# Which engine makes the low halves: two transformer blocks on one core of a Trainium2 chip

## The chip, the cores and the metric

The program runs on one core of one Trainium2 chip, as a single launch. The metric is the device time of the launch in microseconds, the median of several runs. The engines are named as the profile names them: PE (TensorE, matmuls; PEld is its weight load), DVE (VectorE), ACT (ScalarE), POOL (GpSimd) and SP (SyncE, which issues nearly all DMAs).

## What is computed

256 tokens of width 1024 go through three layers, all in float32. Layer one is a chunked gated linear attention and a product-key mixture of experts ("peer"); layer two is a sliding-window attention with sinks and a second peer; layer three adds retention and a latent attention ("mix") and a routed mixture of 32 experts ("moe"). Cut to what matters here:

```python
def first_block(...):
    for l in range(2):
        h = modulate(x, norm_g[l, 0], sh1, sc1)
        y = gla_mixer(h, ...) if l < 1 else swa_sink_attention(h, ...)
        x = x + g1 * y
        y = peer(modulate(x, norm_g[l, 1], sh2, sc2), ...)   # 16384 experts, 8 heads, top 16
        x = x + g2 * y

def token_mixer(u, ...):                        # third layer
    proj = u @ w_in
    rq, rk = apply_rope(rq, *ret_rope), apply_rope(rk, *ret_rope)   # x1*c - x2*s, x2*c + x1*s
    y_ret = (silu(rg) * head_norm(retention(rq, rk, rv))) @ w_ret_o
    y_mla = mla(...) @ w_mla_o
    return (sigmoid(gate_ret) * y_ret + sigmoid(gate_mla) * y_mla) @ w_out
```

## The kernel before

**Low and high halves.** Most large products are made of three matmuls (`mm3`, lines 258 to 260): both operands are split into a high half, which is the float32 value cast to fp32r, and a low half, the float32 rest. Weights come from HBM in pages of 128x1024 (512 KB; some are 512, 704 or 768 wide). `fill` (line 229, through `split`, line 224) loads a page into one of four `raw` buffers; ACT casts it to `hi` (L226), and DVE or POOL subtracts to make `lo` (L227). `hi` and `lo` have three buffers each. So the raw buffer of a page is free, and its successor's load can start, only when the low half is made, and a new page can be cast only when PE is done with the page three before.

**Which engine makes a low half.** `self.lo_every = 2` says that every second page's low half goes to POOL and the other to DVE. In the sums over peer's experts (two loops of 128 pages in each peer layer) the kernel sets it by itself: 0 while POOL scatters gates, 2 otherwise. Everywhere else the initial 2 holds: in the projections of gated attention, of peer's queries, of window attention and of the whole mix.

**The order of work** is written out by hand: the program runs under a manual schedule, so each engine executes its instructions in the order in which the code issues them. `proj_T` and `proj_nat` walk the pages of a weight; at page k they call `page()`, which fills ahead so that pages k+1 and k+2 are split, then issue the matmuls; the last two pages of a projection are taken together. `drive` gives, after each page, one step to a side chain (the attention's small products, rotations, retention) and one `tick` to the background gemv that makes later modulations (L488 and L490 on DVE, buffer `gacc`).

**The other places on POOL.** `affine` (line 422) modulates four 256-column chunks and splits them: for the second bank of a pair DVE casts (L440) and the two low halves with j != k are POOL's (L444). In gated attention POOL makes `kt` (L699). In mix, `turn256` rotates queries and keys: four products on DVE (L1496 to L1499, 128x256) and the difference and sum on POOL (L1500, L1501); `norm` multiplies retention's output by the gate on POOL (L1675, 128x1024); `merge` has POOL make the low halves of the merged activations (L227 with `act<-g`).

Of the kernel before, what the change touches and what calls it, by code (L numbers as in the profile page):

```python
# [10 lines left out]
F32 = mybir.dt.float32  # L11
# [5 lines left out]
OP = mybir.AluOpType  # L17
# [142 lines left out]
class Prog:  # L160
    def __init__(self, ctx, tc, A, pages):
        self.ctx, self.tc, self.A, self.nc = ctx, tc, A, tc.nc
        nc = self.nc
        self.cp = ctx.enter_context(tc.tile_pool(name="cp", bufs=1))
        self.dp = ctx.enter_context(tc.tile_pool(name="dp", bufs=1, space=bass.MemoryType.DRAM))
        self.wp = ctx.enter_context(tc.tile_pool(name="wp", bufs=1))
        self.ps = ctx.enter_context(tc.tile_pool(name="ps", bufs=1, space=PSUM))
        self.pages, self.taken, self.split_at, self.ready = pages, 0, 0, []
        self.landed, self.early = [], 0
        self.lo_every, self.nlo, self.busy = 2, 0, False  # L170
        self.S, self.mc = {}, {}
        self.bg, self.rate, self.credit, self.due = iter(()), 0.0, 0.0, ()
        self.elist, self.eready, self.eat, self.ep, self.rt = list(ELIST), [], 0, {}, None
        self.wr = None
        self.acc, self.gnext, self.graw = None, None, self.raw

        self.gd = [self.dp.tile([128 * 128 * 128, 1], F32, name=f"gd{l}") for l in range(2)]
        self.zq = iter(())
        self.dg, self.s1 = [None, None], [None, None]
        self.ss, self.ss1 = [[None, None] for _ in range(2)], [[None, None] for _ in range(2)]  # L180
        ncol = A["cols"].shape[1]
        self.cols = self.cp.tile([128, ncol], F32, name="cols")
        nc.sync.dma_start(self.cols, A["cols"])
        C = self.cols
        ca = self.cp.tile([128, 16], F32, name="ca")
        nc.scalar.activation(ca, C[:, 0:16], AF.Silu)
        self.cact = self.cp.tile([128, 16, 32], F32, name="cact")
        nc.vector.tensor_copy(self.cact, ca[:, :, None].to_broadcast([128, 16, 32]))
        self.X = self.x8()
        nc.sync.dma_start(self.X, A["x"].rearrange("b p d -> p b d"))  # L190
        self.ident, self.iota = self.const(self.cp, 0, 2)
        self.ng = [[C[:, 16 + 16 * l + 8 * i:24 + 16 * l + 8 * i] for i in range(2)] for l in range(2)]
        self.kvng, self.n1, self.n2 = C[:, 48:56], C[:, 56:64], C[:, 64:72]
        self.qn, self.kvn, self.glan = C[:, 72:75], C[:, 75:77], C[:, 77:79]
        self.fng = C[:, 79:87]
        self.ones = self.cp.tile([128, 128], F32, name="ones")
        nc.vector.memset(self.ones, 1.0)
        self.nhalf = self.cp.tile([128, 8], F32, name="nhalf")
        nc.vector.memset(self.nhalf, -0.5)
        self.rope = self.rope_tab(self.cp)  # L200
# [221 lines left out]
    def affine(self, i, banks, a, sh, hi, lo, nch=8):  # L422

        nc = self.nc
        t = self.tmp()
        at = lambda x, j, k: x[:, (2 * j + k) * 256:(2 * j + k) * 256 + 256]

        def aff(j, k):
            c, o, b = 2 * (i + j) + k, at(t, j, k), banks[j][:, k * 256:k * 256 + 256]
            if j and sh is None:  # L430
                nc.scalar.activation(o, b, AF.Copy, scale=a(c))
            elif j:
                nc.scalar.activation(o, b, AF.Identity, scale=a(c), bias=sh(c))
            elif sh is None:
                nc.vector.tensor_scalar(o, b, a(c), None, op0=OP.mult)
            else:
                nc.vector.tensor_scalar(o, b, a(c), sh(c), op0=OP.mult, op1=OP.add)

        def high(j, k):
            (nc.vector.tensor_copy if j else nc.scalar.copy)(hi[:, 2 * (i + j) + k], at(t, j, k))  # L440

        def low(j, k):
            c = 2 * (i + j) + k
            (nc.gpsimd if j != k else nc.vector).tensor_tensor(lo[:, c], at(t, j, k), hi[:, c].bitcast(F32), OP.subtract)  # L444

        for f, j, k in ((aff, 0, 0), (high, 0, 0), (aff, 1, 0), (aff, 0, 1), (low, 0, 0), (high, 0, 1), (low, 0, 1),
                        (aff, 1, 1), (high, 1, 0), (low, 1, 0), (high, 1, 1), (low, 1, 1)):
            if 2 * (i + j) + k < nch and j < len(banks):
                f(j, k)
# [138 lines left out]
    def gla(self):  # L588
        nc, A, tc = self.nc, self.A, self.tc
        with tc.tile_pool(name="gp", bufs=1) as gp:  # L590
# [14 lines left out]
            hi, lo = act = self.act8(), self.act8()  # L605
# [77 lines left out]
            raw = gp.tile([128, 8, 256], F32, name="qkraw")  # L683
# [12 lines left out]

            def scores():
                nc.vector.scalar_tensor_tensor(qt, raw[:, :4], 128.0 ** -0.5, E[0], op0=OP.mult, op1=OP.mult)
                nc.gpsimd.tensor_tensor(kt, raw[:, 4:], E[1], OP.mult)  # L699
                nc.vector.tensor_tensor(kd, raw[:, 4:], E[2], OP.mult)  # L700
                yield
                kk = gp.tile([128, 4, 128], F32, name="kk")
                for h in range(4):
                    nc.vector.tensor_scalar(kk[:, h, :64], kd[:, h, :64], dec[:, h, 1:2], None, op0=OP.mult)
                    nc.vector.tensor_scalar(qq[:, h, 64:], qt[:, h, 192:], dec[:, h, 2:3], None, op0=OP.mult)
                nc.gpsimd.tensor_copy(kk[:, :, 64:], kd[:, :, 64:128])
                nc.gpsimd.tensor_copy(qq[:, :, :64], qt[:, :, 128:192])
                yield
                pk = self.bank("tp")
                for h in range(4):  # L710
                    nc.tensor.transpose(pk[:, h * 128:h * 128 + 128], kk[:, h], self.ident)
                nc.scalar.copy(kn.rearrange("p a b -> p (a b)"), pk)
                yield
                for tb in range(2):
                    t = slice(tb * 128, tb * 128 + 128)
                    p1, p2 = self.bank("tp"), self.bank("tp")
                    for h in range(4):
                        nc.tensor.matmul(p1[:, h * 128:h * 128 + 128], lhsT=kt[:, h, t], rhs=qt[:, h, t],
                                         start=True, stop=True)
                        nc.tensor.matmul(p2[:64, h * 128:h * 128 + 128], lhsT=kd[:, h, tb * 128:tb * 128 + 64],  # L720
                                         rhs=qt[:, h, t], start=True, stop=True)
                    p1v = p1.rearrange("p (h c) -> p h c", h=4)
                    p2v = p2.rearrange("p (h c) -> p h c", h=4)
                    nc.vector.copy_predicated(sT[:, tb], tri[:, None, :].bitcast(I32).to_broadcast([128, 4, 128]), p1v)
                    nc.vector.tensor_copy(sT[:64, tb, :, 64:], p2v[:64, :, 64:])
                    yield
# [59 lines left out]
    def peer(self, l, mcname, rate=0.0, due=(), fuse=False):  # L786
        nc, A, tc = self.nc, self.A, self.tc
        with tc.tile_pool(name=f"ap{l}", bufs=1) as ap:
# [298 lines left out]
            for i in range(128):  # L1087
# [34 lines left out]
                held = []  # L1122
                self.tick()
            self.acc, self.gnext, self.graw = None, None, self.raw


    def rope_tab(self, pool):
# [229 lines left out]
    def mix(self, due=(), fuse=False):  # L1357
        nc, A, tc = self.nc, self.A, self.tc
        tt = nc.vector.tensor_tensor
        with tc.tile_pool(name="mo", bufs=1) as mo:  # L1360
# [32 lines left out]
            def merge(i):  # L1393
                tt(pair(g2[1], i), bk[i], pair(g2[1], i), OP.mult)
                tt(pair(g2[0], i), pair(g2[0], i), pair(g2[1], i), OP.add)
                self.split(pair(g2[0], i), pair(mh, i), pair(ml, i), nc.gpsimd)

            G = self.gbcast("c2", self.rt.tile([128, 1024], F32, name="G", tag="G"))
            bk = []
# [11 lines left out]
    def branches(self, mi, big, act, oh, ol, gate, due, fuse, rest):  # L1411
# [79 lines left out]
        def turn256(x):  # L1491

            for h in range(4):
                x1, x2 = x[:, 2 * h], x[:, 2 * h + 1]
                w4 = self.tmp().rearrange("p (a t) -> p a t", a=4)
                tt(w4[:, 0], x1, rcos, OP.mult)  # L1496
                tt(w4[:, 1], x2, rsin, OP.mult)
                tt(w4[:, 2], x2, rcos, OP.mult)
                tt(w4[:, 3], x1, rsin, OP.mult)  # L1499
                nc.gpsimd.tensor_tensor(x1, w4[:, 0], w4[:, 1], OP.subtract)  # L1500
                nc.gpsimd.tensor_tensor(x2, w4[:, 2], w4[:, 3], OP.add)  # L1501
                yield

        for dst, side in ((qr, latents()), (kr, turn256(qr))):
# [141 lines left out]
        def retention():  # L1646
# [23 lines left out]
            def norm(nb):  # L1670
                r = self.rstd(mv[:, 4 * nb:4 * nb + 4, 1], 1, 4)
                for h in range(4):
                    nc.vector.tensor_scalar(y[:, nb, h], y[:, nb, h], mv[:, 4 * nb + h, 0:1], r[:, h:h + 1],
                                            op0=OP.subtract, op1=OP.mult)
                nc.gpsimd.tensor_tensor(y[:, nb], y[:, nb], sg[:, nb], OP.mult)  # L1675

            for nb in range(2):
                for h in range(4):
# [408 lines left out]
```

## Time and profile before

| | |
|---|---|
| time of three runs, median | 2559.11 us (2558.82 to 2561.59) |
| profiled execution, its own time | 2556.15 us |
| its span on the core | 2554.1 us, granted TensorE clock 0.98 |
| PE busy | 2383.4 us, 93% |
| DVE, ACT, POOL busy | 64%, 49%, 47% |

The stages by time in the span, from the windows and the lines that belong to each: gated attention 0 to 178, peer's queries to about 216 and its sums to about 1005; window attention to 1140, the second peer's queries to about 1195 and its sums to 1955; mix to 2318, the expert layer to the end. Busy time of an engine counts the time from an instruction's start to its end, so an instruction that stands still inside counts as busy. A wait is put down to the instruction whose end released the one that waited.

### The profile page before, as it was taken

Reading aid. Unit: us, or ns where it says so; the run is one execution under the profiler, and the core shown is the slowest. Engines: PE = TensorE matmul, PEld = TensorE weight load, DVE = VectorE, ACT = ScalarE, POOL = GpSimd, SP = SyncE. Lnnn points to the kernel's source line nnn. Section 1 sums busy time; section 2 is a strip of 40 time slices with the busy share of each in tenths; the row PEclk is TensorE's granted clock in tenths of the full one; section 3 lists DMA queues with packets and bytes.
Section 4 is the critical chain, followed back from the end, with each engine's and each line's share of the span. In section 5 each row is a group of like instructions: output and inputs, shape, how many; then the busy total and the mean of one; then the engine's idle time right before and its main releaser. Section 6 shows DMA issues by size and latency. Waiting matters only on the chain. (4 is left out here: it accounts for less than half of the span.)

```text
span 2554.1 us, 40763 instructions
## 1 busy us (share of the span) xinstructions
PE 2383.4 (93%) x15378; PEld 2034.7 (80%) x15378; DVE 1638.6 (64%) x2884; ACT 1241.8 (49%) x2172; POOL 1194.1 (47%) x676
## 2 busy tenths in 40 slices
PE   7989999999999999889999999999998889798886
PEld 5669999999787877669999999788886878785321
DVE  3772898777478885663898777466665666643211
ACT  2544454698444444554454797444444445332101
POOL 2443487783454544443478774444445543341000
PEclk9999999999999999999999999999999999998999
DMA  8647777765688885548677765688885446588997
GB/s 322 207 168 255 215 185 186 178 149 132 221 306 302 292 314 173 182 155 278 208 189 183 181 141 141 215 273 280 282 286 170 156 161 214 170 334 331 408 409 305
DMA packets 244846, 591.26 MB, mean 231 GB/s; under 512 B 56852, under 2 KB 108948, under 8 KB 244132
## 3 DMA queue, kind: packets, MB, share of 16 engines
q1 hardware_dynamic: 207780, 588.45, 68.3%
q0 software_dynamic: 36864, 0.15, 3.7%
q8 instruction: 123, 2.02, 0.3%
q14 instruction: 79, 0.65, 0.1%
HBM read 568.45 MB, written 20.05 MB: 230 GB/s over the span
## 5 line engine op out<-in xcount | busy, mean ns | idle before, releaser
L226 ACT CAST hi<-raw 128x1024 fp32r<-128x1024 f32 (+3 forms) x690 | 714.4, 1040 | 624.7 <-PE b_acc L260 391.1
L227 POOL TENSOR_TENSOR lo<-raw,hi 128x1024 fp32r<-128x1024 f32 (+2 forms) x238 | 608.8, 2558 | 836.2 <-ACT hi L226 805.3
L227 DVE TENSOR_TENSOR lo<-raw,hi 128x1024 fp32r<-128x1024 f32 (+2 forms) x452 | 589.5, 1305 | 513.0 <-ACT hi L226 496.9
L260 PE MATMUL b_acc<-act,lo 128*128 128x256 f32 x2624 | 748.5, 285 | 20.2 <-POOL lo L227 11.2
L258 PE MATMUL b_acc<-act,hi 128*128 128x256 f32 x2624 | 754.3, 287 | 9.8 <-ACT act L440 4.4
L259 PE MATMUL b_acc<-act,hi 128*128 128x256 f32 x2624 | 746.8, 285 | 2.1 <-DVE act L444 2.0
L954 POOL DMA_INDIRECT gd<-rg x256 | 473.8, 1851 | 133.5 <-issue 73.4
L260 PEld LDWEIGHTS b_acc<-act,lo 128*128 128x128 f32 x2624 | 507.4, 193 | 24.1 <-POOL lo L227 13.3
L258 PEld LDWEIGHTS b_acc<-act,hi 128*128 128x128 f32 x2624 | 507.6, 193 | 13.2 <-ACT act L440 5.1
L259 PEld LDWEIGHTS b_acc<-act,hi 128*128 128x128 f32 x2624 | 507.7, 193 | 2.7 <-DVE act L444 2.7
L259 PE MATMUL b_acc<-lo,act 128*128 128x512 f32 (+1 forms) x1200 | 469.8, 391 | 20.2 <-DVE lo L227 16.0
L258 PE MATMUL b_acc<-hi,act 128*128 128x512 f32 (+1 forms) x1200 | 471.8, 393 | 4.5 <-ACT hi L226 4.4
L260 PE MATMUL b_acc<-hi,act 128*128 128x512 f32 (+1 forms) x1200 | 467.9, 390 | 0.3 <-POOL act L227 0.3
L259 PEld LDWEIGHTS b_acc<-lo,act 128*128 128x128 f32 x1200 | 226.5, 189 | 72.2 <-DVE lo L227 20.7
L258 PEld LDWEIGHTS b_acc<-hi,act 128*128 128x128 f32 x1200 | 226.4, 189 | 62.0 <-issue 8.9
L260 PEld LDWEIGHTS b_acc<-hi,act 128*128 128x128 f32 x1200 | 226.8, 189 | 47.1 <-POOL act L227 0.7
L1058 ACT ACTIVATE A<-b_acc 128x256 f32<-128x256 f32 (+1 forms) x256 | 90.5, 354 | 242.2 <-PE b_acc L260 234.3
L490 DVE SCALAR_TENSOR_TENSOR A<-A,cact 128x1024 f32<-128x1024 f32 x70 | 153.1, 2187 | 3.4 <-DMA A<-in_modw_dram 3.1
L346 POOL TENSOR_TENSOR rs<-rm,nhalf 128x1 f32<-128x1 f32 (+2 forms) x20 | 13.3, 664 | 255.4 <-DVE rm L380 228.7
L1010 ACT ACTIVATE X<-cst,IT 128x128 f32<-128x128 f32 x256 | 88.4, 398 | 0.1
L227 DVE TENSOR_TENSOR act<-A,act 128x1024 fp32r<-128x1024 f32 x62 | 79.8, 1288 | 0.0
L1920 ACT ACTIVATE hd<-b_gv 128x256 f32<-128x256 f32 x8 | 3.1, 384 | 149.8 <-PE b_gv L1918 149.8
(528 smaller groups left out, 2724.9 us busy)
## 6 DMA issues: line engine op xcount, KB each, us to landing
raw<-in_pu_dram SPq DMA_DIRECT2D x256, 512.0 KB
raw<-in_pv_dram SPq DMA_DIRECT2D x256, 512.0 KB
ew<-in_mw_dram SPq DMA_DIRECT2D x87, 512.0 KB
A<-in_modw_dram SPq DMA_DIRECT2D x64, 512.0 KB
raw<-in_win_dram SPq DMA_DIRECT2D x48, 512.0 KB
gr<-in_modw_dram SPq DMA_DIRECT2D x40, 512.0 KB
raw<-in_modw_dram SPq DMA_DIRECT2D x40, 512.0 KB
ez<-in_mw_dram SPq DMA_DIRECT2D x35, 512.0 KB
```

Source lines behind the costliest of these rows:

```text
L226: nc.scalar.copy(hi, src)
L227: (eng or nc.vector).tensor_tensor(lo, src, hi.bitcast(F32), OP.subtract)
L258: nc.tensor.matmul(out, lhsT=lh, rhs=rh, start=start, stop=False, **kw)
L259: nc.tensor.matmul(out, lhsT=lh, rhs=rl, start=False, stop=False, **kw)
L260: nc.tensor.matmul(out, lhsT=ll, rhs=rh, start=False, stop=stop, **kw)
L346: nc.gpsimd.tensor_tensor(y, m, self.nhalf[:, :width], OP.pow)
L490: nc.vector.scalar_tensor_tensor(acc, r, self.cact[:, k, 0:1], acc, op0=OP.mult, op1=OP.add)
L954: d = nc.gpsimd.indirect_dma_start(out=gtab, out_offset=bass.IndirectOffsetOnAxis(ap=row[:, h, j:j + 1], axis=0), in_=gate[:, h, j:j + 1], ...
L1010: nc.scalar.activation(ob[:, 1, j], self.iota, AF.Abs, scale=-1.0, bias=IT[:, 1, t:t + 1])
L1058: nc.scalar.activation(W[:, i, :(128 if tq else 256)], o[:, :(128 if tq else 256)], AF.Gelu)
L1920: nc.scalar.activation(hd[:, 0], b[:, :256], AF.Silu)
```

## The change

Nine lines. `lo_every` starts at 0 and is set back to 0 when a peer layer ends, so that pages outside the two loops over experts have their low half on DVE. In `affine` all casts are ACT's and all low halves DVE's. `kt`, the rotations' difference and sum, retention's gate product and merge's low halves move from POOL to DVE. The loops over experts keep their setting. POOL keeps the root (`pow`), the diagonal for the turned modulation, memsets, small copies and the scatter.

```diff
@@ Prog.__init__
-        self.lo_every, self.nlo, self.busy = 2, 0, False
+        self.lo_every, self.nlo, self.busy = 0, 0, False
@@ affine
         def high(j, k):
-            (nc.vector.tensor_copy if j else nc.scalar.copy)(hi[:, 2 * (i + j) + k], at(t, j, k))
+            nc.scalar.copy(hi[:, 2 * (i + j) + k], at(t, j, k))
         def low(j, k):
             c = 2 * (i + j) + k
-            (nc.gpsimd if j != k else nc.vector).tensor_tensor(lo[:, c], at(t, j, k), hi[:, c].bitcast(F32), OP.subtract)
+            nc.vector.tensor_tensor(lo[:, c], at(t, j, k), hi[:, c].bitcast(F32), OP.subtract)
@@ gla, scores
-                nc.gpsimd.tensor_tensor(kt, raw[:, 4:], E[1], OP.mult)
+                nc.vector.tensor_tensor(kt, raw[:, 4:], E[1], OP.mult)
@@ peer, at its end
             self.acc, self.gnext, self.graw = None, None, self.raw
+            self.lo_every = 0
@@ mix, merge
-                self.split(pair(g2[0], i), pair(mh, i), pair(ml, i), nc.gpsimd)
+                self.split(pair(g2[0], i), pair(mh, i), pair(ml, i))
@@ branches, turn256
-                nc.gpsimd.tensor_tensor(x1, w4[:, 0], w4[:, 1], OP.subtract)
-                nc.gpsimd.tensor_tensor(x2, w4[:, 2], w4[:, 3], OP.add)
+                tt(x1, w4[:, 0], w4[:, 1], OP.subtract)
+                tt(x2, w4[:, 2], w4[:, 3], OP.add)
@@ branches, norm
-                nc.gpsimd.tensor_tensor(y[:, nb], y[:, nb], sg[:, nb], OP.mult)
+                tt(y[:, nb], y[:, nb], sg[:, nb], OP.mult)
```

How this moves instructions, at three places. In the changed program all lines behind the one that was added are higher by one.

DVE at the start of the rotations (`qr` and `kr` are retention's queries and keys, `tm` the four products). Before:

```order
L227 TENSOR_TENSOR lo<-raw,hi 128x1024 x2
L1496 TENSOR_TENSOR tm<-qr,c_19909 128x256
L1497 TENSOR_TENSOR tm<-qr,c_19909 128x256
L1498 TENSOR_TENSOR tm<-qr,c_19909 128x256
L1499 TENSOR_TENSOR tm<-qr,c_19909 128x256
L227 TENSOR_TENSOR lo<-raw,hi 128x1024
```

and with the change:

```order
L227 TENSOR_TENSOR lo<-raw,hi 128x1024 x5
L1497 TENSOR_TENSOR tm<-qr,c_19909 128x256
L1498 TENSOR_TENSOR tm<-qr,c_19909 128x256
L1499 TENSOR_TENSOR tm<-qr,c_19909 128x256
L1500 TENSOR_TENSOR tm<-qr,c_19909 128x256
L1501 TENSOR_TENSOR qr<-tm 128x256
L1502 TENSOR_TENSOR qr<-tm 128x256
L227 TENSOR_TENSOR lo<-raw,hi 128x1024
```

Between two low halves DVE now has six instructions of a rotation; before it had four or eight, and every second low half was on POOL.

DVE in gated attention, where `scores` begins (`qt`, `kt`, `kd` are decayed queries and keys, `gacc` the background gemv), as one piece of the difference:

```order
 L227 TENSOR_TENSOR lo<-raw,hi 128x1024
 L698 SCALAR_TENSOR_TENSOR qt<-qkraw,E_249 128x1024
+L699 TENSOR_TENSOR kt<-qkraw,E_250 128x1024
 L700 TENSOR_TENSOR kd<-qkraw,E_251 128x1024
 L488 TENSOR_SCALAR gacc<-gr,cact 128x1024
+L227 TENSOR_TENSOR lo<-raw,hi 128x1024
 L704 TENSOR_SCALAR kk<-kd,dec 128x64
```

The low half of the next page, which was on POOL, now stands behind `qt`, `kt`, `kd` and a gemv step.

DVE in `merge`, with the change (`act` is the merged activations' low half, cut out of ACT's cast just before it):

```order
L1395 TENSOR_TENSOR g_19900<-b_acc,g_19900 128x512
L1396 TENSOR_TENSOR g_19899<-g_19899,g_19900 128x512
L227 TENSOR_TENSOR act_22297<-g_19899,act_22296 128x512
L1395 TENSOR_TENSOR g_19900<-b_acc,g_19900 128x512
L1396 TENSOR_TENSOR g_19899<-g_19899,g_19900 128x512
L227 TENSOR_TENSOR act_22297<-g_19899,act_22296 128x512
```

Each of the four low halves stands in DVE's queue ahead of the next pair's product; before, DVE went from pair to pair and POOL followed.

Over the whole program 79 low halves of 128x1024 pages and nine narrower ones move from POOL to DVE, with 30 low halves and 30 casts of `affine` (the casts from DVE to ACT), 16 rotation instructions, `kt`, two gate products and four low halves of `merge`.

## Rows read from the trace of the kernel before

**Rows 1.** Busy time by stretch: the sum of nine stretches outside the sums over experts.

```profile
sum 793.00, PE 685.96 PEld 587.54 DVE 458.85 ACT 352.53 POOL 333.46; mean PE 76.22 PEld 65.28 DVE 50.98 ACT 39.17 POOL 37.05
```

**Rows 2.** PE's waits, 2015 to 2080 (rotations, queries): total us, times, longest.

```profile
PE b_acc L260 <- POOL lo L227: 12.0, 4, 3.6
```

**Rows 3.** PE's waits, 2155 to 2240 (retention).

```profile
PE b_acc L260 <- DVE lo L227: 6.6, 4, 4.7
PE b_tp L560 <- POOL t L1675: 3.1, 1, 3.1
PE b_acc L260 <- POOL lo L227: 2.5, 2, 1.3
```

**Rows 4.** PE's waits, 0 to 240 (gated attention, first peer's queries).

```profile
PE b_acc L259 <- DVE lo L227: 3.5, 3, 1.8
...
PE b_acc L260 <- POOL lo L227: 3.0, 3, 1.1
```

**Rows 5.** PE's waits, 1005 to 1195 (window attention, second peer's queries).

```profile
PE b_acc L259 <- DVE lo L227: 4.1, 3, 2.1
PE b_acc L259 <- POOL lo L227: 1.9, 2, 1.5
...
PE b_acc L260 <- DVE lo L227: 1.7, 1, 1.7
```

**Rows 6.** PE's waits, 1955 to 2015 (start of mix).

```profile
PE b_acc L259 <- DVE lo L227: 2.9, 2, 1.9
```

**Rows 7.** Line 227 by engine: durations in ns (least, median, most), first and last start.

```profile
L227 DVE TENSOR_TENSOR lo<-raw,hi x452: 678/1226/3434, 16.4 to 2305.4; 128x1024 fp32r<-128x1024 f32 x148, 128x512 fp32r<-128x512 f32 x1, 128x704 fp32r<-128x704 f32 x1, 128x768 fp32r<-128x768 f32 x1
...
L227 POOL TENSOR_TENSOR lo<-raw,hi x238: 1284/2480/3527, 17.8 to 2302.7; 128x1024 fp32r<-128x1024 f32 x114, 128x512 fp32r<-128x512 f32 x2, 128x704 fp32r<-128x704 f32 x2, 128x768 fp32r<-128x768 f32 x1
```

**Rows 8.** Timeline of DVE and POOL, 2023 to 2030: start, us, instruction, idle before.

```profile
2024.32 2.50 POOL L227 TENSOR_TENSOR lo<-raw,hi 128x1024 fp32r<-128x1024 f32 x1 [4.91 <-ACT hi L226]
2024.47 2.63 DVE L1496 TENSOR_TENSOR tm<-qr,c 128x256 f32<-128x256 f32 x1
2027.36 0.41 DVE L1498 TENSOR_TENSOR tm<-qr,c 128x256 f32<-128x256 f32 x1
...
2028.03 1.21 DVE L227 TENSOR_TENSOR lo<-raw,hi 128x1024 fp32r<-128x1024 f32 x1
```

**Rows 9.** Timeline of ACT, 2270 to 2290 (merge begins at 2279).

```profile
2277.56 1.05 ACT L226 CAST hi<-raw 128x1024 fp32r<-128x1024 f32 x1 [1.78 <-PE b_acc L259]
...
2286.39 0.62 ACT L226 CAST act<-g 128x512 fp32r<-128x512 f32 x1 [1.08 <-DVE g L1395]
```

**Rows 10.** Timeline, 2053 to 2076, DVE and PE (latent attention's queries and keys).

```profile
2053.31 0.96 DVE L227 TENSOR_TENSOR lo<-raw,hi 128x768 fp32r<-128x768 f32 x1 [11.60 <-ACT hi L226]
...
2064.36 0.39 PE L260 MATMUL b_acc<-yh,lo 128*128 128x256 f32 x1 [3.29 <-POOL lo L227]
...
2074.54 0.39 PE L260 MATMUL b_acc<-yh,lo 128*128 128x256 f32 x1 [3.59 <-POOL lo L227]
```

**Rows 11.** Timeline of DVE and POOL, 2174 to 2186 (retention).

```profile
2178.55 0.88 DVE L1655 TENSOR_TENSOR t<-b_tp,c 128x128 f32<-128x128 f32 x4
2179.35 2.82 DVE L490 SCALAR_TENSOR_TENSOR gacc<-raw,cact,gacc 128x1024 f32<-128x1024 f32 x1
2182.09 3.35 DVE L227 TENSOR_TENSOR lo<-raw,hi 128x1024 fp32r<-128x1024 f32 x1
```

**Rows 12.** Timeline, 84 to 98 (gated attention, DVE and PE).

```profile
85.90 2.33 DVE L227 TENSOR_TENSOR lo<-raw,hi 128x1024 fp32r<-128x1024 f32 x1 [3.12 <-ACT hi L226]
...
90.51 0.50 PE L259 MATMUL b_acc<-lo,act 128*128 128x512 f32 x1 [1.27 <-POOL lo L227]
```

**Rows 13.** Line 440 by engine, one of five groups of buffers.

```profile
L440 ACT CAST act<-tm x12: 391/397/407, 24.7 to 1975.9; 128x256 fp32r<-128x256 f32 x12
L440 DVE CAST act<-tm x12: 281/380/858, 25.6 to 1977.2; 128x256 fp32r<-128x256 f32 x12
```

**Rows 14.** Busy time by stretch, 2045 to 2048: PE, PEld, DVE, ACT, POOL, granted clock, DMA.

```profile
2045.00:2048.00 3.00, 3.00 (x16) 3.00 (x16) 0.00 (x0) 0.59 (x1) 1.38 (x1) 0.50 0.75 252
```

## The prediction

> **What bounds the kernel now.** I read the page first, for the share of PE: it is busy 93% of the span, so time can come only from its idle rest and from stretches in which its clock is halved. Then I cut the span at the places where the change ends and begins. The two sums over experts and the last layer are not touched. The nine stretches that are touched last 793 us, in which PE works 686 [rows 1]; the 107 us between are all that any edit here can win back, apart from the clock. Third, the list of PE's waits in these stretches: the reader is to see how much of the 107 us is put down to a low half. It is 12.0 us in the stretch of the rotations and the latent attention's queries [rows 2], 9.1 in retention with 3.1 for the gate product [rows 3], 6.5 in gated attention and the first peer's queries [rows 4], 7.7 in window attention and the second peer's queries [rows 5], 2.9 at the start of mix [rows 6]: 41.3 us together. The rest of the idle time (weights of the first modulation, the diagonals, evacuations) has other causes, which the change leaves alone.
>
> Last, line 227 by engine and a timeline, for the price of a low half and for what the two engines do to each other. A low half lasts 1.23 us on DVE and 2.48 on POOL by the medians [rows 7]. And they do not run side by side: the product of 128x256 that starts 0.15 us behind POOL's low half takes 2.63 us and ends just after it, while two of its like, started with nothing on POOL, take 0.67 from start to start, 0.335 each [rows 8]. So POOL's 2.5 us are taken from DVE wherever DVE has such an instruction to run, and the 3.4 us maxima of both engines [rows 7] are waits of this kind. **DVE and POOL here are one server**, on which POOL is half as fast.
>
> **The change part by part.** DVE gets 79 low halves of 1.2 us, 95 us, and with the smaller moves about 120 us (narrow ones by their width). Its busy time in the stretches is 459 of 793 us [rows 1], part of it standing still behind POOL; even the plain sum, 579, is 73%. DVE does not become the bound on average. What counts is who is late at PE, place by place.
>
> Rotations and queries. A page of 1024 keeps PE 2.83 us (the cast's 1.05 plus its idle 1.78 before PE frees the buffer [rows 9]). Between two low halves DVE now has six instructions of 0.335, so 2.0 + 1.2 = 3.2 us a step: 0.4 too slow for four steps, 1.6 us, which the page and more of lead covers. So the two waits in the keys' projection go: 12.0 less the two shown of 3.29 and 3.59 is 5.1 us [rows 2, 10]. In the queries pages are 768 wide and PE needs only 18 of 24 matmuls, 2.1 us, against DVE's 2.0 + 0.95. Laid end to end from 2053.3 [rows 10]: five low halves of 0.95, four rotations of 2.0, the small rotations between at 2.4 (twelve instructions, 0.2 each by their width), one low half of 1.2, and a page of PE, 2.8: 2072.5. PE was released at 2074.5 [rows 10], so 2.0 us come back. Term: 7.1, between 0 and 12.0.
>
> Retention. DVE's low half that PE waited 4.7 us for ended at 2185.4 [rows 3, 11]. Behind the line-1655 products' start at 2178.55 now come the gate product 1.2, these products 0.8, a gemv step 1.2 and the low half 1.2: 2183.0, 2.4 us earlier. The gate product's own wait of 3.1 shrinks by about 2: 1.2 us on DVE against some 2.5, and no stand behind the gemv. Of the 2.5 us for POOL's low halves I take 2. Term: 6.4, between 0 and 12.2.
>
> Gated attention and the first peer's queries. A loss first: from 85.9 DVE makes a low half, `qt`, `kt` and `kd` (1.2 each), a gemv step of some 0.7 and only then the low half that POOL had made beside it: 92.6. PE wanted it at 90.5 less 1.3, 89.2 [rows 12], and now waits 3.4 instead of 1.3, 2.1 us more. Against it the longest of DVE's waits, 1.8, and two of the 3.0 for POOL [rows 4]. Term: 1.7, between -2.1 and 6.5.
>
> Window attention, the second peer's queries and the start of mix. Here `affine` is in the way. Thirty casts go from DVE to ACT, and ACT has the pages' casts behind them. A cast takes 0.40 on ACT against 0.28 at the least on DVE, and 0.38 at the median, since POOL's low halves run beside it [rows 13]. So ACT hands over the pages' casts some 0.6 us later per call, and DVE's low halves come closer together. I take a third of 7.7 and half of 2.9, so 2.5 and 1.4, between 0 and 10.6 [rows 5, 6].
>
> [...]
>
> Merge. Each low half now waits in DVE's queue for ACT's cast of 0.62 [rows 9], with the next pair's product behind it: four times 0.62, less POOL's longer subtraction, is about 1.3 us later for the casts of the next pages. Term: -1.3.
>
> Clock. [...] Term: 1.5.
>
> The sum is 7.1 + 6.4 + 1.7 + 2.5 + 1.4 - 1.3 + 1.5 = 19.3 us. The profiled execution took 2556.15 us, so 2536.85; the median of the three runs lies 2.96 above that execution, so **2539.8 us**. The bounds: nothing recovered and 3.4 us lost, 2562.5; all 41.3 and the clock recovered and nothing lost, 2516.3.
>
> **The rivals.** *DVE's queue becomes the wait (slower).* One engine in order now carries every low half behind gemv steps, scores, rotations and norms, each waiting for its cast with the rest behind it. It decides wherever more than 2.83 - 1.2 = 1.6 us of other work stands between two low halves and the lead is used up. Were the 2.1 us of `scores` typical of the eleven projections with a side chain on DVE (four in gated attention, two in window attention, two with rotations, two with retention, the merge), that is 23, with 3.2 for eight rotation steps and 1.3 for merge 27.6, against the 22.5 us that PE waits for POOL's products and low halves [rows 2 to 5]: 5 slower, 2564. For it: the piece at 85.9. Against: 73% at most, and POOL's share was never free.
>
> *The wait only changes its name (no change).* The low half waits for ACT's cast, which waits for PE to free the buffer [rows 8, 9]; if this ring sets the pace, the time stays at 2556 to 2561. Against: after a cast of 1.05 POOL's 2.5 us exceed a page, DVE's 1.2 do not.
>
> *All waits on low halves go, and the lower clock behind them (more).* 2516. It needs DVE early everywhere; `scores` and the queries speak against.
>
> **How the numbers follow.** The forecast has 0.66, more 0.12, no change 0.12, slower 0.10. 2516 to 2557 leaves out the slower case, part of the unchanged one and a little beyond the largest gain. A difference of 0.2%, 5.1 us, is about what a measurement of this kernel can tell from none. Faster by more: the forecast and the larger gain, and a little of their lower edge lost, 0.80; within it 0.11; slower 0.09.
>
> **What the profile after would show.** Low halves on DVE at 1.2 us with few above 2 in the touched stretches; `tm` products at 0.41 throughout; no PE wait on POOL's low halves before 216, in 1015 to 1195 or from 1990 on; PE waits on DVE's low halves left near 90, near 2065 to 2072 and at the end of merge; about 20 us less idle on PE, and the sums over experts as long as before. I am wrong if PE's waits on DVE's low halves grow by what POOL's lose, or if waits on ACT's casts or on page loads take their place.

## The result and the profile after

| | before | after |
|---|---|---|
| median of four runs | 2558.97 us (2557.83 to 2561.59) | **2527.6 us** (2523.55 to 2532.59) |
| profiled execution, its own time | 2556.15 us | 2532.59 us |
| its span, PE busy | 2554.1 us, 2383.4 | 2530.3 us, 2383.6 |

The ratio is 0.9878, interval 0.9864 to 0.9893: 31 us faster, where 19.3 were forecast; of the two profiled executions the one after is 23.6 shorter (it is the slowest of its four). Where the time went shows when both spans are cut at the same instructions (the borders are the first transposes, the last copy of the peers' queries, the last copy of the queries that are rotated next, the first copy of the retention's values, the merge's first product and the first expert matmul). Busy time by stretch, before; the columns are the stretch, its length, then busy time and instructions of PE, PEld, DVE, ACT, POOL, the granted clock, DMA:

```profile
175.90:234.70 58.80, 52.28 (x418) 50.47 (x419) 19.83 (x20) 23.32 (x31) 25.34 (x19) 1.00 0.69 226
...
1014.10:1135.00 120.90, 104.29 (x597) 74.39 (x597) 77.97 (x184) 64.50 (x159) 49.11 (x53) 0.97 0.54 171
...
2021.80:2154.20 132.40, 117.66 (x716) 104.27 (x714) 89.70 (x148) 64.01 (x110) 58.20 (x33) 0.96 0.51 168
2154.20:2279.10 124.90, 109.94 (x838) 104.86 (x839) 71.07 (x89) 45.56 (x55) 46.81 (x20) 0.96 0.70 250
2279.10:2334.60 55.50, 49.40 (x248) 39.64 (x248) 30.44 (x85) 20.17 (x36) 21.05 (x20) 0.88 0.78 291
...
sum 2554.10, PE 2383.36 PEld 2034.75 DVE 1638.60 ACT 1241.85 POOL 1194.12; mean PE 216.67 PEld 184.98 DVE 148.96 ACT 112.90 POOL 108.56
```

The same stretches after (first peer's queries, window attention, rotations with the latent attention, retention, merge):

```profile
179.60:233.10 53.50, 53.23 (x418) 52.83 (x419) 24.30 (x28) 24.75 (x36) 2.24 (x7) 0.95 0.73 250
...
1015.30:1134.50 119.20, 104.11 (x596) 74.04 (x596) 80.26 (x196) 66.83 (x167) 17.00 (x33) 0.97 0.55 174
...
2018.40:2139.90 121.50, 115.54 (x716) 103.02 (x714) 90.97 (x181) 63.91 (x110) 0.00 (x0) 0.97 0.59 182
2139.90:2254.20 114.30, 109.10 (x844) 104.11 (x844) 73.46 (x106) 45.31 (x55) 2.03 (x2) 0.97 0.78 275
2254.20:2311.50 57.30, 49.83 (x243) 39.30 (x244) 32.13 (x93) 20.17 (x36) 4.91 (x12) 0.85 0.73 276
...
sum 2530.30, PE 2383.59 PEld 2038.16 DVE 1652.84 ACT 1250.28 POOL 921.77; mean PE 216.69 PEld 185.29 DVE 150.26 ACT 113.66 POOL 83.80
```

Two things are to be seen. In these two executions PE does the same work in the same busy time, so the whole difference between them is idle time of PE. And the two sum rows: POOL lost 272 us of work and DVE, which took it over, is busy only 14 us longer. What it took over would have cost some 120 us; the rest, some 106 us, is time that DVE no longer loses. That it had lost it by standing still behind POOL is what the additions below test. In the rotations' stretch 58 us went from POOL and DVE has 33 instructions more for 1.3 us.

PE's waits after, over the whole run (total, times, longest):

```profile
PE b_acc L259 <- DVE lo L227: 19.2, 18, 4.4
...
PE b_acc L258 <- ACT hi L226: 10.3, 12, 1.8
...
PE b_acc L260 <- DVE lo L227: 7.4, 11, 3.0
...
PE b_acc L258 <- ACT act L440: 6.3, 2, 3.3
...
PE b_acc L258 <- DVE g L1395: 2.9, 2, 1.7
```

And before:

```profile
PE b_acc L259 <- DVE lo L227: 18.8, 15, 2.3
PE b_acc L260 <- POOL lo L227: 18.1, 10, 3.6
...
PE b_acc L260 <- DVE lo L227: 10.3, 10, 4.7
...
PE b_acc L258 <- ACT hi L226: 4.4, 4, 1.3
PE b_acc L258 <- ACT act L440: 4.4, 2, 3.8
PE b_acc L259 <- POOL lo L227: 4.1, 6, 1.5
PE b_tp L560 <- POOL t L1675: 3.1, 1, 3.1
```

The 25 us for POOL are gone but for about 1 us in the sums; waits for DVE's low halves fell by 2.5 in all though DVE makes 88 more of them; ACT's casts are waited for 7.8 us longer. New is one long wait in gated attention and the merge's products.

### The profile page after: what moved, and what is told of

The parts are those of the page before. It is cut to its first block, busy times and chain, and to the rows that moved or that the text cites. A ratio compares the mean times of both kernels' runs of the same rounds, so it can differ in the third digit from the quotient of the medians.

```text
span 2530.3 us, 40726 instructions
## 1 busy us (share of the span) xinstructions
PE 2383.6 (94%) x15378; PEld 2038.2 (81%) x15378; DVE 1652.8 (65%) x2995; ACT 1250.3 (49%) x2202; POOL 921.8 (36%) x535
## 5 line engine op out<-in xcount | busy, mean ns | idle before, releaser
L227 DVE TENSOR_TENSOR lo<-raw,hi 128x1024 fp32r<-128x1024 f32 (+2 forms) x540 | 664.1, 1235 | 498.3 <-ACT hi L226 482.4
L227 POOL TENSOR_TENSOR lo<-raw,hi 128x1024 fp32r<-128x1024 f32 x150 | 387.4, 2583 | 648.8 <-ACT hi L226 595.5
L258 PEld LDWEIGHTS b_acc<-act,hi 128*128 128x128 f32 x2624 | 506.8, 193 | 13.6 <-ACT act L440 7.0
L258 PE MATMUL b_acc<-hi,act 128*128 128x512 f32 (+1 forms) x1200 | 473.7, 395 | 11.2 <-ACT hi L226 8.3
```

The costliest lines, as they stand in the source:

```text
L227: (eng or nc.vector).tensor_tensor(lo, src, hi.bitcast(F32), OP.subtract)
L258: nc.tensor.matmul(out, lhsT=lh, rhs=rh, start=start, stop=False, **kw)
```

## The experiments

The kernel before was timed again in each group of runs (medians 2555.2, 2559.6 and 2557.5 us); every ratio is against the runs beside it.

**Which part of the change.** First the pages' low halves alone; then everything else alone:

```diff
 # pages_only, from the kernel before
-        self.lo_every, self.nlo, self.busy = 2, 0, False
+        self.lo_every, self.nlo, self.busy = 0, 0, False
...
             self.acc, self.gnext, self.graw = None, None, self.raw
+            self.lo_every = 0
 # rest_only, from the kernel after
-        self.lo_every, self.nlo, self.busy = 0, 0, False
+        self.lo_every, self.nlo, self.busy = 2, 0, False
...
-            self.lo_every = 0
```

> The kernel before with one part of the change: the pages' low halves go to VectorE outside the sums over experts; rotations, gate product, kt, the affine casts and the merge stay as before. Theory (VectorE and GpSimd are one server, GpSimd half as fast): most of the gain is here, since 79 instructions of 2.5 us leave GpSimd, but the rotations' 16 products and the small moves still stop VectorE: about 2537, between 2532 and 2542. Rival (GpSimd is only late, VectorE loses nothing to it): the 22 us of waits that name GpSimd go and nothing else, 2537 at the best, with VectorE's waits longer than before by what it takes on. Rival (the gain needs both parts): above 2550.

> The other part alone: rotations' second half, gate product, kt, affine's casts and low halves and the merge's low halves as in the kernel after; the pages' low halves alternate between VectorE and GpSimd as before. Theory (one server): what is moved was half as fast on GpSimd and stopped VectorE, about 40 instructions, few of them on TensorE's path: 2548 to 2556. Rival (GpSimd is only late): the gate product's wait of 3.1 us goes and VectorE, which still has half the pages, gains work: 2556 to 2562. If both parts are independent, the two gains add up to 31 us.

The pages alone took 2524.3 us, ratio 0.9876 (0.986 to 0.9891): the whole of the gain. My 2537 for them was too high. The rest alone took 2547.6, 0.9967 (0.9951 to 0.9983), a gain of about 8. The two are not independent: 1.2% and 0.3% alone, 1.2% together. The stretches of pages_only tell where: its rotations are as long as in the kernel after (121.4 us); its retention takes 116.6 us, 2.3 longer (1.8 than in a second profile of the kernel after), since PE still waits for the gate product on POOL; its merge takes 52.9, 4.3 shorter. So what the other moves win in retention they lose in the merge. PE's wait in pages_only:

```profile
PE b_tp L560 <- POOL t L1676: 2.8, 1, 2.8
```

**Does POOL stop DVE, or is it only late?** To the kernel after, POOL work was added that no one needs, at 33 pages of the mixing: additions (read and write), fills (write), copies (one input).

```diff
+        self.dum = mi.tile([128, 896], F32, name="dum")
+        nc.gpsimd.memset(self.dum, 0.0)
...
-            self.split(r, hi[:, :n], lo[:, :n], nc.gpsimd if pool else nc.vector)
+            cast = self.split(r, hi[:, :n], lo[:, :n], nc.gpsimd if pool else nc.vector)
+            if self.dum is not None and self.nlo % 2:
+                d = nc.gpsimd.tensor_tensor(self.dum, self.dum, self.dum, OP.add).ins
+                self.tc.add_manual_dep(d, cast.name, AFTER, reason="dum")
 # dummy_writes: twice nc.gpsimd.memset(self.dum, 0.0)
 # dummy_copies: twice nc.gpsimd.tensor_copy(self.dum[:, 448:], self.dum[:, :448])
```

> The kernel after, with a GpSimd addition of 896 columns that reads and writes a scratch tile of its own, released by ScalarE's cast of every second page in the last layer's mixing (33 of them, some 2.2 us each, 73 us; nothing waits for them). Theory (one server): VectorE stands still behind each, so low halves come late though all are VectorE's, and much of the 22 us won in the mixing goes back: 2538 to 2550, with VectorE's products of 128x256 up to 2.5 us and TensorE's waits on VectorE's low halves longer. Rival (GpSimd was only late): nothing depends on the additions, so 2524 to 2532 as without them.

> Control to the additions: at the same places GpSimd fills the scratch tile with zeros twice, so it is busy, but reads nothing. Theory (VectorE is stopped where GpSimd's instruction reads SBUF in the way VectorE's two-input ones do): 2524 to 2532, as the kernel after. Rival (any work on GpSimd stops VectorE, or the semaphores and issue slots cost): as with the additions, in proportion to the fills' time.

> The kernel after, with two GpSimd copies of 448 columns inside the scratch tile in place of each addition. The additions cost 30 us, the fills nothing. If reading SBUF is what stops VectorE, copies with one input do it too: 12 to 35 us slower than the kernel after, 2540 to 2562, with products of 128x256 on VectorE well over 0.42 us. If it takes two inputs on GpSimd, as the kernel after: 2523 to 2533.

The additions took 2558.1 us, ratio 1.0005 (0.9995 to 1.0016): the whole gain is given back, more than I had expected, by instructions whose result nothing uses. The fills took 2528.8, 0.99 (0.9885 to 0.9915), as without them; the copies 2538.0, 0.9913 (0.9897 to 0.9929), 12 us more than the kernel after beside them, the least that I gave them if reading is what counts. The mixing from the transposes to the first expert matmul, kernel after, additions, fills, copies (columns as above):

```profile
1962.90:2311.50 348.60, 324.32 (x2134) 293.81 (x2137) 229.23 (x451) 156.01 (x250) 14.01 (x30) 0.94 0.67 226
```

```profile
1960.70:2336.80 376.10, 331.13 (x2130) 297.26 (x2130) 265.45 (x450) 155.98 (x250) 87.97 (x64) 0.94 0.61 209
```

```profile
1954.50:2304.00 349.50, 319.51 (x2130) 288.04 (x2130) 232.58 (x450) 156.05 (x250) 71.19 (x97) 0.96 0.65 225
```

```profile
1958.00:2319.70 361.70, 327.42 (x2130) 294.99 (x2130) 242.20 (x450) 155.91 (x250) 78.65 (x97) 0.94 0.63 218
```

With the same instructions DVE is busy 36 us longer beside 74 us of additions, and the mixing lasts 27.5 us longer, 20.7 of them idle time of PE; 3 us and 0.9 with 57 us of fills; 13 and 13 with 65 us of copies. Where DVE loses it, additions first, is the timeline of the rotations:

```profile
2029.18 1.90 DVE L1504 TENSOR_TENSOR tm<-qr,c 128x256 f32<-128x256 f32 x1
2031.00 0.41 DVE L1505 TENSOR_TENSOR tm<-qr,c 128x256 f32<-128x256 f32 x1
```

with POOL in the same place, where two additions end at 2030.80 and the product at 2031.08,

```profile
2025.52 5.28 POOL L251 TENSOR_TENSOR dum<-dum 128x896 f32<-128x896 f32 x2 [7.17 <-ACT hi L227]
```

and with the fills the first of the same products, while two fills of 1.75 us together are under way:

```profile
2014.14 0.42 DVE L1505 TENSOR_TENSOR tm<-qr,c 128x256 f32<-128x256 f32 x1
```

```profile
2014.23 1.75 POOL L252 MEMSET dum<- 128x896 f32 x2 [0.53 <-ACT hi L227]
```

PE's waits for what POOL itself makes in the mixing are the same in all four (6.3 us for a diagonal, 0.8 for a copy), so POOL's own work behind the additions is not what came late. That settles it for the mixing: POOL's reading of SBUF, not its lateness and not its being busy, is what cost: 36 us of DVE's time beside 74 us of additions and 13 beside 65 of copies, which read, 3 beside 57 of fills, which do not; in the rows above 1.90 us for a product beside an addition, 0.42 beside fills.

**What the change lost, and what it left.** Four runs on the places where the profile after still shows a price.

```diff
 # merge_back
-                self.split(pair(g2[0], i), pair(mh, i), pair(ml, i))
+                self.split(pair(g2[0], i), pair(mh, i), pair(ml, i), nc.gpsimd)
 # scores_split
+                yield
                 nc.vector.tensor_tensor(kt, raw[:, 4:], E[1], OP.mult)
+                yield
                 nc.vector.tensor_tensor(kd, raw[:, 4:], E[2], OP.mult)
 # sums_on_vector
-                self.lo_every = 0 if todo or sent else 2
+                self.lo_every = 0
...
-            self.lo_every = 2
```

> The kernel after with the merge's four low halves on GpSimd again, as before. Theory (each of them on VectorE waits for ScalarE's cast with the next pair's product behind it): from the merge's first product to the first expert matmul 57.3 us became 55.5 or less, and the whole 2 to 4 us faster than the kernel after, which took 2527.6 against 2559.0 (ratio 0.9878): ratio about 0.9865. Rival (the stretch only carries waits over from before it): no difference.

> The kernel after with gated attention's three products qt, kt, kd set apart by a page each instead of in one piece. Theory (four instructions of 1.2 us and a gemv step stand ahead of a low half on VectorE and TensorE waits 4.4 us for it): that wait shrinks to under 1.5, gated attention ends about 3 us earlier than 179.6, unless the chain of scores, two pages later now, becomes what the end waits for. Rival (the start's loss is ScalarE's casts, not VectorE's queue): the wait goes to another place and the transposes behind gated attention begin at 178 to 180 as in the kernel after.

> The kernel after with the low halves inside the two sums over experts on VectorE too: no page's low half is left on GpSimd. By the theory (one server, GpSimd half as fast) this can't be slower in the sums: 150 low halves of 2.58 us on GpSimd become 1.23 on VectorE; TensorE has only 27 us of idle time in the sums, 10 of it waits for low halves, so 0 to 10 us faster than the kernel after, and VectorE stays under nine tenths busy. Rival (in the sums GpSimd's share is needed, VectorE's queue there has the top-k and the gates): slower than the kernel after by 5 or more, with TensorE's waits on VectorE's low halves grown.

> Both the merge's low halves on GpSimd and gated attention's products set apart. If the two are independent and each does what the theory says, 5 to 7 us faster than the kernel after: ratio to before about 0.985 to 0.9858.

The merge took 2524.7 us, 0.9863 (0.984 to 0.9886), an interval that holds the kernel after too. The stretch tells more: 54.4 us against 57.3, and 52.9 to 54.9 in the four kernels that have the pages on VectorE and these halves on POOL, 55.6 to 57.8 in the seven profiles with both on VectorE. PE's idle time in it parts them more clearly: 4.9 to 5.3 us in the four, 7.4 to 7.8 in the seven. The stretch in merge_back:

```profile
2248.90:2303.30 54.40, 49.50 (x239) 39.51 (x237) 30.74 (x88) 20.11 (x36) 11.21 (x16) 0.84 0.77 290
```

The scores took 2521.0, 0.9857 (0.9832 to 0.9881): the wait of 4.4 us is one of 2.0, where I had expected less than 1.5, and the transposes begin at 175.8 us, in the other two kernels with this edit at 173.9 and 171.7, against 177.1 to 179.6 in seven profiles with the products in one piece. PE's wait in scores_split:

```profile
PE b_acc L259 <- DVE lo L227: 2.0, 1, 2.0
```

Both together 2521.0, 0.9844 (0.9821 to 0.9867), no less than the scores alone: the whole time can't tell the merge's 2 to 3 us. The sums took 2514.7, 0.9828 (0.9806 to 0.985), 13 us below the kernel after, a little more than the 0 to 10 that I gave them. First sum over experts, from the last copy of the queries, after and then this kernel:

```profile
233.10:1015.30 782.20, 767.32 (x4975) 695.94 (x4973) 604.39 (x1031) 438.14 (x756) 440.99 (x209) 0.99 0.75 222
```

```profile
232.40:1001.00 768.60, 761.33 (x4975) 692.77 (x4974) 604.96 (x1106) 439.05 (x756) 240.29 (x134) 1.00 0.75 226
```

75 low halves more on DVE, 92 us at 1.23, and its busy time is the same: what it takes over, it stops losing. Of the 13.6 us, 7.6 are idle time of PE; 6 are PE's own time, at a granted clock of 1.00 instead of 0.99. That these 6 come from the edit is not shown: in pages_only, with the instructions of the kernel after in this sum, PE's own time is 762.7 us too, and the sum 776.0. The second sum, after and then this kernel, says less for the edit:

```profile
1187.40:1962.90 775.50, 763.42 (x4959) 694.73 (x4957) 546.24 (x1010) 441.38 (x764) 430.80 (x214) 0.99 0.74 214
```

```profile
1171.50:1945.40 773.90, 762.65 (x4959) 694.94 (x4958) 586.94 (x1085) 441.81 (x764) 242.85 (x139) 0.99 0.74 215
```

Here 75 more low halves make DVE 41 us busier, so it stops losing little more than half of what it takes over, and the sum is 1.6 us shorter.

Last, all three edits, and the kernel after once more:

> The kernel after with three edits together: the low halves of the sums over experts on VectorE (alone 2514.7 us), gated attention's products set apart (alone 2521.0) and the merge's four low halves on GpSimd (alone 2524.7). Theory (they act in different places and add): the sums give 10 to 12 us against the kernel after, the products 3, the merge 2 to 3: 2509 to 2513, ratio to before about 0.981. Rival (the gains are the same idle time counted more than once): no faster than 2514.7.

> The kernel after itself, unchanged, for a second profile beside the others. If the sums over experts with the first peer layer's weights lost 4 us to the change (1015.3 - 205.7 = 809.6 against 1014.1 - 208.7 = 805.4), they last 809 to 810 again; if that is scatter between executions, 803 to 807, and the whole 2523 to 2528.

All three took **2506.3 us**, 0.9798 (0.9785 to 0.9812), a little under the 2509 to 2513 expected: the gains add, and this version beats both kernels. The kernel after took 2526.1, 0.9869 (0.9854 to 0.9885). Its first sum, from the border that the expectation uses (the first copy of the queries), took 810.4 us, what was expected if the change costs 4 us there. But in the eight other kernels with the same instructions in the sums it took 803.4 to 807.1, and the kernel before, profiled once, 805.4. So whether the change costs 4 us there is not settled.

## Why the prediction was right

Direction and mechanism held, and the larger sizes were too small. Length of the stretch before and after, in the profile after and in the one taken again:

| stretch | before | after | again | gain | forecast |
|---|---|---|---|---|---|
| gated attention, first peer's queries | 234.7 | 233.1 | 230.8 | 1.6, 3.9 | 1.7 |
| window attention, second peer's queries | 176.4 | 172.1 | 170.2 | 4.3, 6.2 | 2.5 |
| start of mix | 55.9 | 55.5 | 55.6 | 0.4, 0.3 | 1.4 |
| rotations, queries, latent attention | 132.4 | 121.5 | 121.2 | 10.9, 11.2 | 7.1, clock 1.5 |
| retention | 124.9 | 114.3 | 114.8 | 10.6, 10.1 | 6.4 |
| merge | 55.5 | 57.3 | 57.2 | -1.8, -1.7 | -1.3 |

The stretches won 26.0 us together, 30.0 in the second profile; the first sum over experts, which the forecast left as it was, took 2.8 and 3.6 us more.

- **One server.** Right for what POOL did here, and shown by the additions (74 us, 36 of DVE's time); the fills (57 us, 3 of DVE's time) show a limit that the prediction did not have, that POOL must read SBUF. What was sized too small is what DVE gets back by it. "With the smaller moves about 120 us" and "the plain sum, 579, is 73%" counted the work that DVE gets, and only named the time that it stood still. Measured, DVE's busy time rose by 14 us in all. I priced the waits of PE's list one by one, and gave back half of retention's 12.2 us and 60% of the 12.0 of the rotations. Of the 12.2 us 3.1 are left, of the 12.0 3.5.
- **Rotations and queries.** The keys' waits (5.1 us, [rows 2] less those in [rows 10]) went but for 0.3, the products take 0.42 us throughout. Up to the last copy of the keys that are rotated 6.5 us came back, as forecast: 5.1, and 1.5 for the clock. Behind it 4.4 came back, where I had 2.0: of the queries' two waits [rows 10] the second, 3.6, went altogether, and the first is still 3.0.
- **Retention.** The 4.7 us [rows 3] became 1.0, and the gate product's wait is gone instead of 1.1 left. From the gate product to the end of the low half DVE took 4.35 us, where I had laid out 4.4. But I had started from the time before the change, as if nothing ahead of it had been held up; the normalisation's line 359, a few instructions earlier, had lasted 2.33 us beside a low half on POOL. Before and after:

```profile
2172.98 2.33 DVE L359 TENSOR_SCALAR rm<-mv 128x4 f32<-128x4 f32 x1
```

```profile
2159.81 0.16 DVE L359 TENSOR_SCALAR rm<-mv 128x4 f32<-128x4 f32 x1
```

- **Gated attention.** The loss at `scores` was right in place and near in size: the low half that I laid end to end over 6.7 us took 6.6 (timeline of DVE, below), and PE waited 4.4 us, 3.4 by the forecast. Gated attention ends 3.7 us later (2.0 in the second profile) and the queries behind it take 5.3 less (5.9); forecast were 2.1 lost and 3.8 won.

```profile
87.02 1.23 DVE L227 TENSOR_TENSOR lo<-raw,hi 128x1024 fp32r<-128x1024 f32 x1 [3.13 <-ACT hi L226]
...
92.24 1.42 DVE L227 TENSOR_TENSOR lo<-raw,hi 128x1024 fp32r<-128x1024 f32 x1
```

- **Casts.** In window attention and the queries behind it PE's waits for low halves fell from 8.2 us, the 7.7 of [rows 5] and a small one, to 1.2, and those for ACT's casts of pages grew from 1.2 to 4.6, as forecast. Still 4.3 to 6.2 us came back, not a third of 7.7. That the thirty casts of `affine` cost it anything is not shown: pages_only, which leaves them on DVE, won 4.7 in the same stretch.
- **Merge.** Right: the timeline of DVE shows four low halves like this one, each after 0.69 us of waiting for the cast, 2.8 us less what POOL's subtraction took longer. PE's idle time in the stretch grew by 1.4 us (6.1 to 7.5), 1.3 by the forecast.

```profile
2256.32 0.69 DVE L227 TENSOR_TENSOR act<-g,act 128x512 fp32r<-128x512 f32 x1 [0.69 <-ACT act L226]
```

- **Clock.** The forecast's 1.5 us was my estimate from 3 us at a granted clock of 0.50 [rows 14]; no run shows the term by itself. The runs show that this stretch went, and that from the last copy of the queries to the last of the keys the granted clock rose from 0.94 to 1.00 and PE's own time fell by 1.8 us. Before and after:

```profile
2021.80:2052.00 30.20, 25.08 (x195) 24.67 (x193) 18.23 (x20) 10.33 (x13) 18.27 (x12) 0.94 0.40 126
```

```profile
2018.40:2042.00 23.60, 23.26 (x194) 23.06 (x193) 17.32 (x32) 10.30 (x12) 0.00 (x0) 1.00 0.51 151
```

In the whole it did not count: PE's busy time is the same (2383.4 and 2383.6), since as much was lost elsewhere, at the start of mix among others (48.0 us of PE's time became 49.9). In the second profile of the kernel after it is 2379.7, so executions of one kernel differ by more than the term.

Of the rivals, DVE's queue as the new bound is real in two places, some 3 and 2 us, which scores_split and merge_back gave back; a third is the queries' wait of 3.0 us, which no run touched. The ring that would only rename the wait fell: the waits for ACT's casts grew by 8 us, not by 25. All waits gone, 2516, lay 11 us below the median; two of the kernels above went past it, by way of the sums, which the change does not touch.

## What to carry to other kernels

Where POOL helps DVE with elementwise work out of SBUF, count its time against DVE too: here 74 us of additions on POOL cost DVE 36 us, and taking over 272 us of POOL's work cost it 14. Look for DVE instructions that last several times as long as their like, here 1.90 us against 0.42 beside an addition and 2.33 against 0.16 beside a low half; their excess is what POOL, nominally free, took away here. What cost almost nothing here on POOL is what reads nothing (57 us of fills cost DVE 3), and a low half whose input comes late was better off DVE's queue than in it (the merge, by some 2.5 us of PE's idle time).

## What the hardware showed that I had not expected

Fills on POOL did not stretch DVE's two-input products of the rotations (0.42 us in both kernels), but did stretch some instructions with one input, from 0.41 to 1.01 us. Retention's normalisation, the kernel after and then the one with fills (ns: least, median, most):

```profile
L1674 DVE TENSOR_SCALAR t<-t,mv,rs x8: 406/408/413, 2161.9 to 2186.8; 128x256 f32<-128x256 f32 x8
```

```profile
L1682 DVE TENSOR_SCALAR t<-t,mv,rs x8: 395/406/1015, 2153.6 to 2180.9; 128x256 f32<-128x256 f32 x8
```

The two that took 1.01 us are the two that ran beside fills. Why these were stretched and the products not, no run here shows. It was too seldom to show in the time: 2528.8 us with the fills, 2526.1 and 2527.6 without. And copies on POOL, with a single input, stopped DVE as well, though by less: products of 0.42 us took up to 0.78, beside copies of 0.67 (median).
